# Sums of log f as spread rows, a stacked rank-17 product, a step inside the log sigmoid, and one product for two stacked heads

## The chip, the core and the metric

The kernel runs on one core of a Trainium2 chip. The metric is the device time of one execution in microseconds (us); lower is better. Engines are named as the profile names them: PE is TensorE (matmul), PEld its weight load, DVE is VectorE, ACT is ScalarE, POOL is GpSimd, SP is SyncE, which issues most of the DMA transfers.

## The reference, cut to what matters

Two layers of a decoder trunk over 256 positions of width 2048. Each layer normalises, projects to the columns of four head groups (four heads of width 128 each), runs four kinds of attention, gates them and maps back; a last RMSNorm follows. The change touches the forgetting attention, the gate of the gated linear attention (GLA) and GLA's product across chunks.

```python
log_f = jax.nn.log_sigmoid((p["fox_f"] + fox_fb).astype(jnp.float32)).transpose(0, 2, 1)
# forgetting attention: logit[t, s] = q_t.k_s / sqrt(d) + F[t] - F[s], F = cumsum(log f), causal
cum = jnp.cumsum(log_f.astype(jnp.float32), axis=-1)
logits = jnp.einsum("bhqd,bhkd->bhqk", q_i, k, preferred_element_type=jnp.float32) * scale
logits = logits + c_i[..., :, None] - cum[:, :, None, :]
...
# gated linear attention: the gate's logits are a product of rank 16 plus a bias (17 rows)
a_logit = jnp.einsum("bsr,re->bse", p["gla_a"], gla_wa2) + gla_ba
log_a = jax.nn.log_sigmoid(a_logit.astype(jnp.float32)) / GLA_TAU
```

The softmax takes no notice of a term that is the same for all keys of a row, so only the part of the sums that changes with the key `s` has to be added to the scores.

## The kernel before

**The stream.** All weights come in a list of steps, `plan`. For each step SP loads 512 or 348 KB into one of four buffers (`raw`); ScalarE writes the high part (`hi`, float32r), VectorE the rest (`lo = raw - hi`), and TensorE multiplies hi and lo with the high and low parts of the transposed activations (`hTp`, later `mTh` and `mTl`): `mm` is the usual PSUM tile of these products, `side` one of two PSUM tiles for everything else. The parts are made three steps ahead (`prepare`, `PART_BUFS` 4). A step of 512 columns is eight products with hi and four with lo.

**The side work.** Attention, norms and transposes are Python generators in the list `tasks`. After each step `tick` lets them run, one `yield` at a time, as long as the estimated time of VectorE and ScalarE (`Costed`) stays under what the products of the step give; so a piece of code between two `yield`s is issued together, and the order of all engines is fixed when the program is built. A key in `ready` tells one task that another has issued its result. Slots `s4` (ten tiles of 128x1024), `s2` (six of 128x512) and `s8` are handed out in the same way.

**log f.** `gla_gate` reads the four columns `fox_f` of both query blocks into `fx` and starts `fox_forget`: VectorE adds the bias, `log_sigmoid` runs Abs, Exp and Ln on ScalarE, and VectorE subtracts. `f` is split into `fh` and `fl`; ScalarE scales the constant triangles `since` by each head's column into two tiles of 128x1024. In `softmax_part` the object `forget` (class `Forget`) puts two products of a matrix of ones (`ones_r`) with these tiles in front of the score products of each key block, so the sums along the keys arise in PSUM.

**The gate.** `gla_first` reads the 16 columns `gla_a` into `an`; `gla` transposes them on TensorE, VectorE copies 16 rows into `at17`, whose row 17 holds ones, and two float32 products with `wa` (17 rows: `gla_wa2` and `gla_ba`) give the logits, which `log_sigmoid` takes further.

**GLA across chunks.** For each pair of heads, `ee[:, 0, NL]` and `ee[:, 1, NL]` hold the decayed k and q of two heads, 64 rows each; two products on rows 0 to 63 and 64 to 127 give `px`.

**The first norm.** `first_rms` squares the transposed x, adds it up into two tiles (`xts[0]`, `xts[3]`), and for each query block two products with a column of ones add up both.

`turned` is the pattern by which a tile is turned: VectorE transposes squares of 32, SP writes to the far memory (`far`), POOL reads back, and `LANDS` = 4 yields pass before the tile is used.

Of the kernel before, what the change touches and what calls it, by code (L numbers as in the profile page):

```python
# [208 lines left out]
def hybrid_trunk(  # L209
# [140 lines left out]
    wa = cp.tile([17, DEPTH, 256], F32, name="wa")  # L350
    ones_r = cp.tile([P, P], F32R, name="ones_r")
# [3 lines left out]
    at17 = cp.tile([17, SEQ], F32, name="at17")  # L355
# [17 lines left out]
    nc.vector.memset(at17, 1.0)  # L373

    def constants():
# [3 lines left out]
        nc.scalar.dma_start(wa[0:16], gla_wa2.rearrange("l r e -> r l e"))  # L379
        nc.scalar.dma_start(wa[16:17].rearrange("p l e -> p (l e)"), gla_ba.rearrange("(o l) e -> o (l e)", o=1))  # L380
# [15 lines left out]
        v_.tensor_scalar(ones_r, ident, 0.0, 1.0, op0=OP.mult, op1=OP.add)  # L396
        s4.put(mb)
        ready.add("constants")
# [131 lines left out]
    def log_sigmoid(dst, xin, e):  # L530

        a_.activation(e, xin, AF.Abs)
        a_.activation(e, e, AF.Exp, scale=-1.0)
        a_.activation(e, e, AF.Ln, bias=1.0)
        yield
        v_.scalar_tensor_tensor(dst, xin, 0.0, e, op0=OP.min, op1=OP.subtract)


    def gla_first(l, ps):
        r = env["r", l]  # L540
        an = sm.tile([P, 2, 16], F32, name="an", bufs=2)
        sg = sgs.get([P, 2, GW])
        env["gla_sg", l] = sg
        for m in range(2):
            a_.activation(an[:, m], ps[m][:, 0:16], AF.Copy, scale=r[:, m:m + 1])
            a_.activation(sg[:, m, :332], ps[m][:, 16:], AF.Silu, scale=r[:, m:m + 1])
        tasks.append(gla(l, an))
# [22 lines left out]
    def gla_gate(l, ps):  # L570
# [8 lines left out]
        env["forget", l] = Forget()  # L579
        tasks.append(fox_forget(l, fx, env["forget", l]))  # L580
# [11 lines left out]
    def gla(l, an):  # L592
        yield from until("constants")
        ps = yield from take_side()
        for m in range(2):
            transpose(ps[0:16, m * P:(m + 1) * P], an[:, m])
        yield
        v_.tensor_copy(at17[0:16], ps[0:16, 0:256])
        side.put(ps)
        yield  # L600
        al = yield from take_side()
        for pair in range(2):
            matmul(al[:, pair * SEQ:(pair + 1) * SEQ], wa[:, l, pair * P:(pair + 1) * P], at17, True, True)
# [21 lines left out]
        for pair in range(2):  # L625
# [34 lines left out]
            v_.tensor_mul(ee[:, 1, NL], ee[:, 1, NL], qv[:, 1])  # L660
# [19 lines left out]
            for hh in range(2):  # L680
                rows = slice(hh * 64, hh * 64 + 64)
                matmul(px[:, hh * 512:hh * 512 + P], ee[rows, 0, NL], ee[rows, 1, NL], True, True, tiles=2)
            s8.put(ee)
            yield
            a_.activation(sx[:, pair * 2:pair * 2 + 2], px.rearrange("p (h t) -> p h t", h=2)[:, :, :P], AF.Copy)
# [19 lines left out]
    def softmax_part(m, qT, kT, rows, scale, su, forget=None):  # L705
# [3 lines left out]
        for kt in range(m + 1):  # L709
            dst = S[:, kt]  # L710
            if forget is not None:
                forget(dst, kt)
            for h in range(H):
                matmul(dst[:, h], qT[rows, m * H + h], kT[1][rows, kt * H + h],
                       forget is None, forget is None or h == H - 1)
        yield
        v_.tensor_add(S[:, m], S[:, m], neg4)
        mx = sm.tile([P, H], F32, name="mx")
# [25 lines left out]
    def attend(l, gi, name, qT, kT, forget=None):  # L744
# [4 lines left out]
        for m, pool in enumerate((s2, s4)):  # L749
            p = yield from softmax_part(m, qT, kT, slice(0, P), HD ** -0.5, su, forget)  # L750
            if m:
                s4.put(qT, kT[0])
                if forget is not None:
                    forget.release()
# [40 lines left out]
    class Forget:  # L795

        def __init__(self):
            self.fg = []  # L800

        def __call__(self, dst, kt):
            matmul(dst, ones_r, self.fg[0][:, kt], True, False)
            matmul(dst, ones_r, self.fg[1][:, kt], False, False)

        def release(self):
            s4.put(*self.fg)

# [6 lines left out]
    def fox_forget(l, fx, forget):  # L815
        yield
        v_.tensor_add(fx, fx, fb[:, l, None, :].to_broadcast([P, 2, H]))
        e = sm.tile([P, 2, H], F32, name="fe", bufs=2)
# [4 lines left out]
        fh = sm.tile([P, 2, H], F32R, name="fh", bufs=2)  # L823
        fl = sm.tile([P, 2, H], F32R, name="fl", bufs=2)
        hi_of(fh, f)
        lo_of(fl, f, fh)
# [475 lines left out]
```

## Time and profile before

| | before |
|---|---|
| median of 3 runs | 910.66 us (910.32 to 911.14) |
| the profiled execution | 910.05 us |
| its span, first to last instruction | 908.3 us |
| mean granted clock of TensorE | 0.997 |
| instructions: PE, DVE, ACT, POOL | 4489, 833, 827, 55 |
| DMA queues: the share of 16 engines that SP's queue (q1) takes | 61.5% |
| table loads on ScalarE | 26 of 1.28 us under the helper's line, 1 at the start |

In the timeline of the profile a row is a run of like instructions on one engine: start, duration, engine, line, operation, tiles written and read, weights' shape, moving shape, count, and in brackets the idle time ahead and what ended it. The duration of a run of products includes the filling of the array, so the distance from one start to the next is what it takes from the stream. A float32 product appears as two records in the trace, a float32r product as one. Nearly all lines are those of helpers (L277 `matmul`, L179 the costed call), so groups are told apart by their tiles.

### The profile page before, as it was taken

How to read it: one execution, taken by the hardware profiler on the slowest of the kernel's cores; microseconds unless marked ns; L12 is line 12 of the kernel's file. 1: busy time of each engine (PE TensorE's matmuls, PEld its weight loads, DVE VectorE, ACT ScalarE, POOL GpSimd, SP SyncE). 2: the span in 40 equal slices, each digit the busy share in tenths (PEclk: the TensorE clock that was granted, in tenths of full speed). 3: DMA queues.
4: the chain of work that ended last, by engine and by line, in shares of the span. 5: the costliest groups of instructions: out<-in, count | busy, mean ns of one | idle time of the engine just before them, and what ended most of it. 6: DMA issues, size and time to landing. Idle time of an engine off the chain costs nothing.

```text
span 908.3 us, 12430 instructions
## 1 busy us (share of the span) xinstructions
PE 898.7 (99%) x4489; PEld 765.0 (84%) x4489; DVE 570.2 (63%) x833; ACT 530.9 (58%) x827; POOL 36.3 (4%) x55
## 2 busy tenths in 40 slices
PE   9999999999999999999999999999999999999996
PEld 7988889888888888888899888988888888888886
DVE  6764878466668555646655568766655684665662
ACT  7678654654656555535565785547645644754451
POOL 0000000000000010000000000000000000110000
PEclk9999999999999999999999999999999999999998
DMA  8857767479656947858776466674967588497652
GB/s 280 271 209 247 253 195 249 143 240 337 230 189 211 315 146 238 293 189 273 222 233 213 147 235 205 188 239 139 346 232 233 176 260 282 151 309 270 183 176 93
DMA packets 77743, 205.34 MB, mean 226 GB/s; under 512 B 9297, under 2 KB 29425, under 8 KB 77682
## 3 DMA queue, kind: packets, MB, share of 16 engines
q1 hardware_dynamic: 70640, 183.42, 61.5%
q0 software_dynamic: 5408, 19.40, 6.0%
q10 hardware_dynamic: 1634, 1.73, 0.6%
q8 instruction: 35, 0.57, 0.3%
q14 instruction: 26, 0.21, 0.1%
HBM read 184.07 MB, written 20.45 MB: 225 GB/s over the span
## 4 chain that ended last, share of the span: by engine, by line
PE 97%; ACT 1%; issue 1%; DVE 0%; POOLq 0%; POOL 0%; DVEq 0%; ACTq 0%
PE mm L277 87%; PE side L277 10%; PE side L369 0%; ACT L179 0%; ACT hi L179 0%; ACT two L179 0%; DVE two L179 0%; DVE xs L179 0%; POOLq L1298 0%; ACT four L179 0%; POOL rf L424 0%; ACT fe L179 0%; DVEq L1298 0%; PE side L281 0%; ACT gate L179 0%
## 5 line engine op out<-in xcount | busy, mean ns | idle before, releaser
L179 DVE TENSOR_TENSOR lo<-raw,hi 128x1024 fp32r<-128x1024 f32 (+2 forms) x319 | 368.0, 1160 | 299.9 <-ACT hi L179 288.4
L179 ACT ACTIVATE hi<-raw 128x1024 fp32r<-128x1024 f32 (+2 forms) x319 | 319.6, 1009 | 295.5 <-PE mm L277 231.0
L277 PE MATMUL mm<-hi,hTp 128*128 128x512 f32 (+1 forms) x1920 | 461.1, 382 | 0.6 <-ACT hi L179 0.6
L277 PEld LDWEIGHTS mm<-hi,hTp 128*128 128x128 f32 x1920 | 351.1, 188 | 66.1 <-ACT hi L179 2.2
L277 PE MATMUL mm<-lo,hTp 128*128 128x512 f32 (+1 forms) x960 | 248.1, 380 | 0.0
L277 PEld LDWEIGHTS mm<-lo,hTp 128*128 128x128 f32 x960 | 177.4, 188 | 32.8
L277 PE MATMUL mm<-hi,mTh 128*128 128x512 f32 (+1 forms) x256 | 64.6, 377 | 0.0
L277 PE MATMUL mm<-hi,mTl 128*128 128x512 f32 (+1 forms) x256 | 64.4, 376 | 0.0
L277 PE MATMUL mm<-lo,mTh 128*128 128x512 f32 (+1 forms) x256 | 64.4, 376 | 0.0
L277 PEld LDWEIGHTS mm<-lo,mTh 128*128 128x128 f32 x256 | 46.2, 188 | 8.8
L277 PEld LDWEIGHTS mm<-hi,mTl 128*128 128x128 f32 x256 | 46.2, 188 | 8.8
L277 PEld LDWEIGHTS mm<-hi,mTh 128*128 128x128 f32 x256 | 46.1, 188 | 8.6
L313 POOL DMA_DIRECT2D four<-far x32 | 17.2, 539 | 598.9 <-DMA far<-four 243.4
L277 PE MATMUL side<-four,four 128*128 128x128 f32 (+1 forms) x320 | 37.0, 276 | 0.0
L277 PEld LDWEIGHTS side<-four,four 128*128 128x128 f32 (+1 forms) x320 | 34.1, 190 | 2.3 <-issue 1.4
L179 ACT ACT_TABLE_LOAD x26 | 33.4, 1283 | 0.4
L179 DVE STREAM_TRANSPOSE four<-four 128x1024 f32<-128x1024 f32 x24 | 29.5, 1231 | 0.0
L179 ACT ACTIVATE four<-mm,rstd 128x512 f32<-128x512 f32 (+1 forms) x40 | 24.4, 661 | 0.1
L277 PE MATMUL side<-hi,hTp 128*128 128x348 f32 x128 | 23.1, 321 | 0.0
L277 PEld LDWEIGHTS side<-hi,hTp 128*128 128x128 f32 x128 | 20.9, 188 | 1.4 <-issue 0.7
L179 ACT ACTIVATE four<-side,nb 128x256 f32<-128x256 f32 (+1 forms) x48 | 20.5, 439 | 1.3 <-DVE nb L179 1.2
L179 ACT ACTIVATE four<-side 32x64 f32<-32x64 f32 (+2 forms) x28 | 8.8, 342 | 18.2 <-PE side L277 17.9
(135 smaller groups left out, 498.5 us busy)
## 6 DMA issues: line engine op xcount, KB each, us to landing
raw<-in_weights SPq DMA_DIRECT2D x271, 512.0 KB, 4.3
far<-four SPq DMA_DIRECT2D x128, 128.0 KB, 4.4
four<-far POOLq DMA_DIRECT2D x32, 512.0 KB, 5.9
raw<-in_weights SPq DMA_DIRECT2D x46, 348.0 KB, 3.7
xs<-in_x SPq DMA_DIRECT2D x4, 512.0 KB, 5.0
four<-in_xt SPq DMA_DIRECT2D x3, 512.0 KB, 5.8
far<-two SPq DMA_DIRECT2D x24, 64.0 KB, 4.2
two<-far POOLq DMA_DIRECT2D x6, 256.0 KB, 5.3
```

The source lines that it names most:

```text
L179: return f(*args, **kw)
L277: t_.matmul(out, lhsT, rhs, start=start, stop=stop)
L313: g_.dma_start(t, d.rearrange("j c i f -> (j c) (i f)"))
```

## The change

Six edits. (1) The sums of log f: two products of `f` with the triangles give one row of sums per head (4 rows); VectorE copies them, SP writes them to the far memory, POOL reads them back spread over all 128 partitions into one tile, and VectorE adds this tile to the scores. The class `Forget`, `ones_r` and the 32 scaled copies go. (2) The rank-17 product: `an` holds the 16 columns and a one three times, in strips of 32; the product is one float32r product over 128 rows, with strips high·high, low·high and high·low. (3) A `yield` between VectorE's addition and Abs, one between Exp and Ln, and more of them around the sums and the gate. (4) GLA's two products become one of 256 columns whose moving tile `qx` has zeros where the rows belong to the other head. (5) The first norm adds both tiles on VectorE and needs one product for each query block. (6) Memsets of the new tiles, and six transfers for `wa`'s strips instead of two.

```diff
@@ -349,4 +349,3 @@
     gng = cp.tile([P, DEPTH], F32, name="gng")
-    wa = cp.tile([17, DEPTH, 256], F32, name="wa")
-    ones_r = cp.tile([P, P], F32R, name="ones_r")
+    wa = cp.tile([P, DEPTH, 256], F32R, name="wa")
     neg_b = cp.tile([P, P], BF16, name="neg_b")
@@ -354,3 +353,5 @@
     halfpow = cp.tile([P, 8], F32, name="halfpow")
-    at17 = cp.tile([17, SEQ], F32, name="at17")
+    at = cp.tile([P, SEQ], F32R, name="at")
+    an = cp.tile([P, 2, 4, 32], F32, name="an")
+    qx = cp.tile([P, 2, P], F32, name="qx")
     lam = cp.tile([P, DEPTH], F32, name="lam")
@@ -372,3 +373,2 @@
     keep_warm(WARM)
-    nc.vector.memset(at17, 1.0)
 
@@ -378,4 +378,7 @@
         nc.scalar.dma_start(ct, const)
-        nc.scalar.dma_start(wa[0:16], gla_wa2.rearrange("l r e -> r l e"))
-        nc.scalar.dma_start(wa[16:17].rearrange("p l e -> p (l e)"), gla_ba.rearrange("(o l) e -> o (l e)", o=1))
+        w3 = s2.get([P, DEPTH, 256])
+        g_.memset(w3, 0.0)
+        for i in range(0, 96, 32):
+            nc.scalar.dma_start(w3[i:i + 16], gla_wa2.rearrange("l r e -> r l e"))
+            nc.scalar.dma_start(w3[i + 16:i + 17].rearrange("p l e -> p (l e)"), gla_ba.rearrange("(o l) e -> o (l e)", o=1))
         yield
@@ -395,4 +398,7 @@
         v_.tensor_copy(masks.rearrange("p l t -> p (l t)"), mb)
-        v_.tensor_scalar(ones_r, ident, 0.0, 1.0, op0=OP.mult, op1=OP.add)
         s4.put(mb)
+        hi_of(wa, w3)
+        yield
+        lo_of(wa[64:96], w3[64:96], wa[64:96])
+        s2.put(w3)
         ready.add("constants")
@@ -533,2 +539,3 @@
         a_.activation(e, e, AF.Exp, scale=-1.0)
+        yield
         a_.activation(e, e, AF.Ln, bias=1.0)
@@ -540,3 +547,2 @@
         r = env["r", l]
-        an = sm.tile([P, 2, 16], F32, name="an", bufs=2)
         sg = sgs.get([P, 2, GW])
@@ -544,5 +550,5 @@
         for m in range(2):
-            a_.activation(an[:, m], ps[m][:, 0:16], AF.Copy, scale=r[:, m:m + 1])
+            a_.activation(an[:, m, 0:3, 0:16], ps[m][:, None, 0:16].to_broadcast([P, 3, 16]), AF.Copy, scale=r[:, m:m + 1])
             a_.activation(sg[:, m, :332], ps[m][:, 16:], AF.Silu, scale=r[:, m:m + 1])
-        tasks.append(gla(l, an))
+        tasks.append(gla(l))
 
@@ -578,4 +584,3 @@
         env["fox_v", l] = vn
-        env["forget", l] = Forget()
-        tasks.append(fox_forget(l, fx, env["forget", l]))
+        tasks.append(fox_forget(l, fx))
 
@@ -591,3 +596,3 @@
 
-    def gla(l, an):
+    def gla(l):
         yield from until("constants")
@@ -595,10 +600,12 @@
         for m in range(2):
-            transpose(ps[0:16, m * P:(m + 1) * P], an[:, m])
+            transpose(ps[:, m * P:(m + 1) * P], an[:, m].rearrange("p a r -> p (a r)"))
         yield
-        v_.tensor_copy(at17[0:16], ps[0:16, 0:256])
+        v_.tensor_copy(at, ps[:, :SEQ])
+        lo_of(at[32:64], ps[32:64, :SEQ], at[32:64])
         side.put(ps)
         yield
+        yield
         al = yield from take_side()
         for pair in range(2):
-            matmul(al[:, pair * SEQ:(pair + 1) * SEQ], wa[:, l, pair * P:(pair + 1) * P], at17, True, True)
+            matmul(al[:, pair * SEQ:(pair + 1) * SEQ], wa[:, l, pair * P:(pair + 1) * P], at, True, True)
         yield
@@ -659,3 +666,5 @@
             v_.tensor_mul(ee[:, 0, NL], ee[:, 0, NL], kv[:, 0])
-            v_.tensor_mul(ee[:, 1, NL], ee[:, 1, NL], qv[:, 1])
+            for hh in range(2):
+                rows = slice(hh * 64, hh * 64 + 64)
+                v_.tensor_mul(qx[rows, hh], ee[rows, 1, NL], qv[rows, 1])
             yield
@@ -679,8 +688,6 @@
             px = yield from take_side()
-            for hh in range(2):
-                rows = slice(hh * 64, hh * 64 + 64)
-                matmul(px[:, hh * 512:hh * 512 + P], ee[rows, 0, NL], ee[rows, 1, NL], True, True, tiles=2)
+            matmul(px[:, :2 * P], ee[:, 0, NL], qx.rearrange("p h t -> p (h t)"), True, True)
             s8.put(ee)
             yield
-            a_.activation(sx[:, pair * 2:pair * 2 + 2], px.rearrange("p (h t) -> p h t", h=2)[:, :, :P], AF.Copy)
+            a_.activation(sx[:, pair * 2:pair * 2 + 2], px[:, :2 * P].rearrange("p (h t) -> p h t", h=2), AF.Copy)
             side.put(px)
@@ -709,10 +716,8 @@
         for kt in range(m + 1):
-            dst = S[:, kt]
-            if forget is not None:
-                forget(dst, kt)
             for h in range(H):
-                matmul(dst[:, h], qT[rows, m * H + h], kT[1][rows, kt * H + h],
-                       forget is None, forget is None or h == H - 1)
+                matmul(S[:, kt, h], qT[rows, m * H + h], kT[1][rows, kt * H + h], True, True)
         yield
         v_.tensor_add(S[:, m], S[:, m], neg4)
+        if forget is not None:
+            v_.tensor_add(S[:, :m + 1], S[:, :m + 1], forget[:, :m + 1])
         mx = sm.tile([P, H], F32, name="mx")
@@ -753,3 +758,3 @@
                 if forget is not None:
-                    forget.release()
+                    s4.put(forget)
             v_.reciprocal(rs[:, m], su[:, m])
@@ -794,16 +799,2 @@
 
-    class Forget:
-
-
-
-        def __init__(self):
-            self.fg = []
-
-        def __call__(self, dst, kt):
-            matmul(dst, ones_r, self.fg[0][:, kt], True, False)
-            matmul(dst, ones_r, self.fg[1][:, kt], False, False)
-
-        def release(self):
-            s4.put(*self.fg)
-
     def fox_v(l, ps):
@@ -814,5 +805,6 @@
 
-    def fox_forget(l, fx, forget):
+    def fox_forget(l, fx):
         yield
         v_.tensor_add(fx, fx, fb[:, l, None, :].to_broadcast([P, 2, H]))
+        yield
         e = sm.tile([P, 2, H], F32, name="fe", bufs=2)
@@ -822,15 +814,21 @@
         yield
-        fh = sm.tile([P, 2, H], F32R, name="fh", bufs=2)
-        fl = sm.tile([P, 2, H], F32R, name="fl", bufs=2)
-        hi_of(fh, f)
-        lo_of(fl, f, fh)
-        yield
-        for part in (fh, fl):
-            z = yield from s4.take([P, 2, H, P], F32R)
-            pf = part.bitcast(F32)
-            for m in range(2):
-                for h in range(H):
-                    a_.activation(z[:, m, h], since[m], AF.Copy, scale=pf[:, m, h:h + 1])
-            forget.fg.append(z)
+        yield
+        yield
+        ps = yield from take_side()
+        for m in range(2):
+            matmul(ps[:H, m * P:(m + 1) * P], f[:, m], since[m], True, True)
+        yield
+        c = sm.tile([H, 2, P], F32, name="cum", bufs=2)
+        v_.tensor_copy(c, ps[:H, :SEQ].rearrange("h (m s) -> h m s", m=2))
+        side.put(ps)
+        yield
+        d = yield from far.take([1, 2, H, P])
+        nc.sync.dma_start(d[0].rearrange("m h s -> h m s"), c)
+        yield
+        z = yield from s4.take([P, 2, H, P])
+        g_.dma_start(z.rearrange("p m h s -> p (m h s)"), d.rearrange("o m h s -> o (m h s)").to_broadcast([P, 2 * H * P]))
+        far.put(d)
+        for _ in range(LANDS):
             yield
+        env["forget", l] = z
         ready.add(("forget", l))
@@ -1147,2 +1145,3 @@
                 fold(xts[0 if c == 2 else 3])
+        v_.tensor_add(xts[0][:, 0], xts[0][:, 0], xts[3][:, 0])
         yield
@@ -1151,4 +1150,3 @@
         for m in range(2):
-            for c in (0, 3):
-                matmul(ps[:, m:m + 1], xts[c][:, 0, m * P:(m + 1) * P], one, c == 0, c == 3)
+            matmul(ps[:, m:m + 1], xts[0][:, 0, m * P:(m + 1) * P], one, True, True)
         t = before_pow(ps[:, 0:2], 2, 1.0 / D)
@@ -1249,2 +1247,5 @@
     g_.memset(tq, 0.0)
+    g_.memset(qx, 0.0)
+    g_.memset(an, 0.0)
+    g_.memset(an[:, :, 0:3, 16:17], 1.0)
     tasks += [constants()]
```

Three places show how the order moves. On TensorE in the first layer, the gate (`an` transposed by `ct`, then `at` with `wa`) before:

```order
L281 MATMUL side_612<-ct,an 16x128 x2
L277 MATMUL mm<-hi,hTp 128x512 x8
L277 MATMUL mm<-lo,hTp 128x512 x4
L277 MATMUL side_210<-hi,hTp 128x348 x8
L277 MATMUL side_210<-lo,hTp 128x348 x4
L277 MATMUL side_661<-at_91,wa 128x256 x2
```

and now:

```order
L281 MATMUL side_638<-ct,an 128x128 x2
L277 MATMUL side_213<-hi,hTp 128x348 x8
L277 MATMUL side_213<-lo,hTp 128x348 x4
L277 MATMUL side_213<-hi,hTp 128x348 x8
L277 MATMUL side_213<-lo,hTp 128x348 x4
L277 MATMUL mm<-hi,hTp 128x512 x8
L277 MATMUL mm<-lo,hTp 128x512 x4
L277 MATMUL side_725<-at,wa 128x256 x2
```

The product with `wa` moves behind a step of 512 columns, and the transposes fill 128 rows instead of 16.

On TensorE in the first layer, the scores of the forgetting attention for the second query block (`four,ones_r` are the rows of log f, `four,four` queries and keys) before:

```order
L277 MATMUL mm<-lo,hTp 128x512 x4
L277 MATMUL side_1771<-four_823,ones_r 128x512
L277 MATMUL side_1771<-four_850,ones_r 128x512
L277 MATMUL side_1771<-four_1404,four_1312 128x128 x4
L277 MATMUL side_1771<-four_823,ones_r 128x512
L277 MATMUL side_1771<-four_850,ones_r 128x512
L277 MATMUL side_1771<-four_1404,four_1312 128x128 x4
```

and now, with the score products of the first query block ten rows ahead:

```order
L277 MATMUL side_1569<-four_1374,four_1322 128x128 x4
L277 MATMUL mm<-hi,hTp 128x512 x8
L277 MATMUL mm<-lo,hTp 128x512 x4
L277 MATMUL mm<-hi,hTp 128x512 x8
L277 MATMUL mm<-lo,hTp 128x512 x4
L277 MATMUL mm<-hi,hTp 128x512 x8
L277 MATMUL mm<-lo,hTp 128x512 x4
L277 MATMUL mm<-hi,hTp 128x512 x8
L277 MATMUL mm<-lo,hTp 128x512 x4
L277 MATMUL side_1672<-four_1374,four_1322 128x128 x8
```

The rows of ones are gone, the score products stand together, and four steps instead of five lie between the two query blocks.

On ScalarE in the second layer, the log sigmoid of log f (`fx` to `fe`: Abs, Exp, Ln) among the high parts before:

```order
L179 ACTIVATE four_4444<-side_4043,rstd 128x164
L179 ACTIVATE hi<-raw 128x1024
L179 ACTIVATE fe<-fx 128x8
L179 ACT_TABLE_LOAD
L179 ACTIVATE fe<-fe 128x8
L179 ACT_TABLE_LOAD
L179 ACTIVATE fe<-fe 128x8
L179 ACTIVATE hi<-raw 128x1024 x2
L179 ACTIVATE fh<-f 128x8
```

and now, with the end of the gate's log sigmoid (`two`) ahead of it:

```order
L179 ACTIVATE two_4452<-two_4452 128x512
L179 ACTIVATE hi<-raw 128x1024
L179 ACT_TABLE_LOAD
L179 ACTIVATE two_4452<-two_4452 128x512
L179 ACTIVATE hi<-raw 128x1024
L179 ACTIVATE fe<-fx 128x8
L179 ACT_TABLE_LOAD
L179 ACTIVATE fe<-fe 128x8
L179 ACTIVATE hi<-raw 128x1024
L179 ACT_TABLE_LOAD
L179 ACTIVATE fe<-fe 128x8
L179 ACTIVATE hi<-raw 128x1024 x3
```

A high part now stands between Exp and Ln of either log sigmoid.

## The prediction

> **What bounds the kernel now.** I read the page's head first, then the chain that ended last, then what TensorE and ScalarE waited for, and last TensorE's timeline around each place that the change touches.
>
> ```profile
> span 908.3 us, 12430 instructions
> PE 898.7 (99%) x4489; PEld 765.0 (84%) x4489; DVE 570.2 (63%) x833; ACT 530.9 (58%) x827; POOL 36.3 (4%) x55
> PE 97%; ACT 1%; issue 1%; DVE 0%; POOLq 0%; POOL 0%; DVEq 0%; ACTq 0%
> PE mm L277 <- ACT hi L179: 0.6, 1, 0.6
> ACT hi L179 <- PE mm L277: 231.0, 155, 3.9
> ```
>
> TensorE is busy 99% of the span and carries 97% of the chain. Once the projections run, the only wait of TensorE is one of 0.6 us, while ScalarE waits 231.0 us for TensorE before it may write the next high part. So the time is the length of TensorE's instruction stream: what leaves it is gained in full, what joins it is paid in full, and work on the other engines is free until a weight part comes late. A busy time overlaps its neighbours, so I take every price from start to start. The rhythm of a step is the unit:
>
> ```profile
> 508.66 1.98 PE L277 MATMUL mm<-hi,hTp 128*128 128x512 f32 x8
> 510.47 1.07 PE L277 MATMUL mm<-lo,hTp 128*128 128x512 f32 x4
> 511.38 1.98 PE L277 MATMUL mm<-hi,hTp 128*128 128x512 f32 x8
> ```
>
> Eight products take 1.81 us and four take 0.91: a step of twelve is 2.72 us. Where a group of four or eight takes longer than that, the insertion beside it is charged with the excess.
>
> **The rows of log f (TensorE, both layers).** Before, each key block of the scores begins with two products of the ones matrix.
>
> ```profile
> 164.54 0.64 PE L277 MATMUL side<-four,ones_r 128*128 128x512 f32 x2
> 165.02 1.05 PE L277 MATMUL side<-four,four 128*128 128x128 f32 x8
> ...
> 179.55 0.64 PE L277 MATMUL side<-four,ones_r 128*128 128x512 f32 x2
> ...
> 180.84 0.71 PE L277 MATMUL side<-four,ones_r 128*128 128x512 f32 x2
> ...
> 182.19 2.09 PE L277 MATMUL mm<-hi,hTp 128*128 128x512 f32 x8
> 333.64 1.95 PE L277 MATMUL side<-four,four 128*128 128x128 f32 x16
> 335.35 2.10 PE L277 MATMUL mm<-hi,hTp 128*128 128x512 f32 x8
> ```
>
> For the first query block they take 165.02 - 164.54 = 0.48 us. For the second, the whole group takes 182.19 - 179.55 = 2.64; the MoBA scores of the same shape, which have no such rows, take 335.35 - 333.64 = 1.71 for their 16 instructions. So 0.48 + 0.93 = 1.41 a layer goes, **-2.8 us** in two. In their place come two float32 products with 4-column weights and 128 moving columns a layer. No row has that form. Each float32 product is two instructions here (eight scores, 16 records); at 1.71 / 16 = 0.107, and 0.111 with the 0.04 lost at the group's edge, four cost 0.45 to 0.5: **+1.0 us**. The bounds are 4 x 0.07 (a transpose with few columns, below) and 4 x 0.26 (the dearest float32 row below): +0.6 to +2.1.
>
> The rest of this part leaves TensorE. The 32 scaled copies on ScalarE go; VectorE gets an addition of the table to the scores, 512 and 1024 elements wide. The same engine adds the mask at 0.69 us for 512, so a layer pays 0.69 + about 1.4 = 2.1:
>
> ```profile
> L179 DVE TENSOR_TENSOR side<-side,neg_b 128x512 f32<-128x512 f32 x12 | 8.3, 692 | 5.5 <-PE side L277 5.5
> far<-four SPq DMA_DIRECT2D x128, 128.0 KB, 4.4
> two<-in_final_norm_g POOLq DMA_DIRECT2D x4, 256.0 KB, 9.5
> ```
>
> I cost it at nothing: VectorE is idle 37% of the span and in each step has 2.72 us for one low part. If that cover were gone, 4.2 us would join the path. The addition also waits for the table's round trip, 4.4 us to the far memory and, as a spread row, some 9.5 to twice that back: 14 to 23 us. Queued behind it on VectorE are the low parts. But between the copy of the sums and the addition stand 25 low parts in VectorE's order, one a step, some 68 us. On SP's queue the write of the sums stands between weight loads, and waits for a VectorE copy made one turn earlier; the turned tiles' writes stand there in the same way today. On POOL's queue the spreading read stands between two reads like it.
>
> **The rank-17 product.**
>
> ```profile
> 500.89 1.42 PE L277 MATMUL side<-hi,hTp 128*128 128x348 f32 x8
> 502.15 0.79 PE L277 MATMUL side<-lo,hTp 128*128 128x348 f32 x4
> 502.87 1.13 PE L277 MATMUL side<-at,wa 17*128 17x256 f32 x4
> 503.93 1.52 PE L277 MATMUL side<-hi,hTp 128*128 128x348 f32 x8
> 505.29 0.79 PE L277 MATMUL side<-lo,hTp 128*128 128x348 f32 x4
> 895.14 0.28 PE L277 MATMUL side<-four,mTl 128*128 128x256 f32 x1
> 895.26 0.40 PE L277 MATMUL side<-four,mTh 128*128 128x256 f32 x2
> 895.50 0.28 PE L277 MATMUL side<-four,mTl 128*128 128x256 f32 x1
> ```
>
> Two float32 products, four instructions, take 503.93 - 502.87 = 1.06 us (0.26 each). They also stretch their neighbours: eight of 348 columns take 1.26 ahead and 1.36 behind, and the four between take 0.72 where half of 1.26 is 0.63. Together 1.25. After, there are two float32r products with 256 moving columns and 128 rows, one instruction each; three such take 895.50 - 895.14 = 0.36, so two take 0.24. That is 1.0 a layer, **-2.0 us**. The bounds: if the new product kept the old price per instruction, 2 x 0.26, it would be -1.5.
>
> The transposes ahead of it now load 128 columns of weights instead of 16, and the square sums of the first norm lose one of two products:
>
> ```profile
> 46.40 0.95 PE L277 MATMUL side<-one,four 128*128 128x1 f32 x8
> 47.21 1.50 PE L277 MATMUL mm<-hi,hTp 128*128 128x348 f32 x8
> 51.92 0.38 PE L281 MATMUL side<-ct,an 128*16 128x128 f32 x2
> 52.06 2.07 PE L277 MATMUL mm<-hi,hTp 128*128 128x512 f32 x8
> ```
>
> Eight square-sum instructions take 47.21 - 46.40 = 0.81, so half is **-0.4 us**. Two transposes take 0.14; with full weights I give each the 0.10 of a square-sum instruction, which has full weights and one moving column: 0.20, **+0.1 us** in two layers. The Trainium skill ("TensorE: Matmul & The Clock Gate", LDWEIGHTS) prices a weight load by its columns at 1.2 per ns, 107 ns for 128 against 13 for 16; by that the two layers would pay about 0.4. The trace agrees for full weights: the square-sum instructions come every 0.10 us.
>
> **The stacked rows' product.** Two products on 64 rows become one on 128 rows, whose other half is zeros, with twice the columns.
>
> ```profile
> 116.93 1.08 PE L277 MATMUL mm<-lo,hTp 128*128 128x512 f32 x4
> 117.94 0.49 PE L277 MATMUL side<-eight 64*128 64x128 f32 x4
> 118.36 2.11 PE L277 MATMUL mm<-hi,hTp 128*128 128x512 f32 x8
> 120.31 1.07 PE L277 MATMUL mm<-lo,hTp 128*128 128x512 f32 x4
> 250.42 1.16 PE L277 MATMUL side<-four,four 64*128 64x128 f32 x16
> 251.51 2.11 PE L277 MATMUL mm<-hi,hTp 128*128 128x512 f32 x8
> ```
>
> Before, the pair takes 118.36 - 117.94 = 0.42, the four ahead 1.01 instead of 0.91 and the eight behind 1.95 instead of 1.81: 0.66. After, two instructions of 256 columns at twice 0.111, with 0.04 for the edge: 0.48. Four pairs: **-0.7 us**; at 0.26 each it is -0.4.
>
> Against this edit speaks a rule of the Trainium skill ("TensorE: Matmul & The Clock Gate", Part 3): small products on different row groups run at the same time, and a short contraction costs as much as a full one. The trace agrees where the run is long: 16 instructions of 64 rows take 251.51 - 250.42 = 1.09, or 0.068 each against 0.107. What it does here is a rival below.
>
> **The step between the instructions (and the queues).** The one wait of TensorE is at 520:
>
> ```profile
> 518.63 1.07 PE L277 MATMUL mm<-lo,hTp 128*128 128x512 f32 x4
> 520.25 2.12 PE L277 MATMUL mm<-hi,hTp 128*128 128x512 f32 x8 [0.56 <-ACT hi L179]
> 516.00 0.21 ACT L179 ACTIVATE fe<-fx 128x8 f32<-128x8 f32 x1 [2.69 <-DVE fx L179]
> 519.16 1.99 ACT L179 ACTIVATE hi<-raw 128x1024 fp32r<-128x1024 f32 x2
> ```
>
> ScalarE stood 2.69 us at Abs, waiting for VectorE's addition, then ran Abs, Exp and Ln with two table loads up to 519.16, and only then wrote the high part that TensorE needed. In the new order a high part stands on either side of Exp and ahead of Abs, and the addition is issued a turn ahead of Abs. Four of the group took 1.62 us instead of 0.91: **-0.7 us** if nothing takes its place. What is late next is the high part after the two table loads of the rank-17 product's log sigmoid; there too a high part now stands between the loads. The constants issue four more transfers on ScalarE's queue near 40 us, some 2 us by their spacing in the trace (0.5), where ScalarE later idles 2.0 us for TensorE: nothing.
>
> **Sum:** -2.8 + 1.0 - 2.0 - 0.4 + 0.1 - 0.7 - 0.7 = **-5.5 us**. The profiled execution took 910.05 us, 1.75 more than its span; 904.5 follows for one like it. The median of the three runs is 0.61 higher, so I forecast **905.1 us**.
>
> **Rivals.**
> 1. *A new late part.* The side work now starts several steps earlier in the stream, as the order shows, and ScalarE's or VectorE's burst may meet a due part elsewhere. For it: a wait of 0.56 already cost 0.7. Against it: ScalarE loses 32 copies and four table loads. The gain of 0.7 stays out and one or two waits come at 0.7 each: 906 to 907.
> 2. *The 64-row pairs were cheap.* If two products overlapped wholly, as the long run suggests, and the edges came from elsewhere, a pair cost 4 x 0.068 = 0.27 and its successor 0.48: +0.8 instead of -0.7, 906.6. This is what the Trainium skill's rule above gives here ("TensorE: Matmul & The Clock Gate", Part 3).
> 3. *The change does not do what it says on TensorE:* the stacked product and the sums' product run at 0.26 an instruction. The first loses 0.5 and the second adds 1.1: 906.7.
> 4. *Slower: the spread table comes late.* VectorE stands at the addition with the low parts behind it. TensorE has three steps ahead, 8 us. To lose the 4.8 us that the other terms give (5.5 less the 0.7 at 520), each layer must wait 2.4 us beyond these 8, so the table must land 68 + 8 + 2.4 = 78 us after the copy. The round trip is 14 to 23. If it took 85, the time would be 910.66 - 4.8 + 2 x 9 = 924.
>
> **How the numbers follow.** Forecast 0.62, rival 1 0.15, rival 2 0.10, rival 3 0.05, rival 4 0.04; 0.04 is left for a gain that other waits eat up to within 0.2% (1.8 us), about what a measurement of this kernel can tell from no change. The kind end of the sums' products, +0.6, gives 904.7, and the runs of before lie up to 0.5 from their median: from 904.1 down to 904.0. Rivals 1 to 3 end at 907, with the same spread 907.4. The range 904.0 to 907.4 leaves out rival 4, the rest and a little on either side. Faster 0.91, same 0.05, slower 0.04.
>
> **What would show it.** The ones rows gone from the groups and MoBA-like groups of 8 and 16 in the FoX scores; groups for the sums at 0.45 to 0.5 a layer; two products of 256 columns in 0.24; a 256-column product of the stacked rows in 0.45; no wait of TensorE on ScalarE near 520. I am wrong if TensorE's waits exceed 1 us in sum, if VectorE waits for the table, or if the sums' products take more than 0.7 us.

## The result and the profile after

The changed kernel takes **905.56 us** (median of four runs, 905.17 to 906.74) against 910.77 for the kernel before on the same chip (910.32 to 911.14): a ratio of 0.9945, with a 95% interval of 0.9928 to 0.9962, so 5.2 us less. The profiled execution of the changed kernel took 906.74 us (span 905.0), the slowest of its four; the one of before took 910.05. What the two traces differ by, 3.3 us, is therefore less than what the medians differ by, and a part of the reading below is why.

The head of the page after (busy time and share of each engine, then the shares of the chain that ended last):

```profile
span 905.0 us, 12378 instructions
PE 894.0 (99%) x4469; PEld 762.8 (84%) x4469; DVE 579.2 (64%) x843; ACT 518.0 (57%) x790; POOL 40.3 (4%) x61
PE 97%; DMA 1%; issue 1%; DVE 0%; ACT 0%; ACTq 0%; POOLq 0%; POOL 0%; DVEq 0%; SPq 0%
```

TensorE still sets the time: 99% busy, 97% of the chain. ScalarE lost 13 us of work and VectorE gained 9, and neither shows in the chain. What TensorE waited for (in total, times, longest):

```profile
PE side L277 <- DVE four L179: 1.3, 1, 1.3
PE side L370 <- DVE one L365: 1.2, 1, 1.2
PE mm L277 <- ACT hi L179: 0.2, 1, 0.2
```

The second row is the warm-up before the first projection, at the start of the span; before had the same. The third is the first projection's own start: 0.24 us at 5.45, where only the warm-up had run. The first is new. TensorE's timeline (start, duration, line, operation, and in brackets the idle time ahead) at the places that the change touches:

```profile
46.19 0.79 PE L277 MATMUL mm<-lo,hTp 128*128 128x348 f32 x4
48.26 0.58 PE L277 MATMUL side<-one,four 128*128 128x1 f32 x4 [1.28 <-DVE four L179]
48.70 1.51 PE L277 MATMUL mm<-hi,hTp 128*128 128x348 f32 x8
...
81.32 1.07 PE L277 MATMUL mm<-lo,hTp 128*128 128x512 f32 x4
82.32 0.60 PE L277 MATMUL side<-ct,f 128*4 128x128 f32 x4
82.85 2.11 PE L277 MATMUL mm<-hi,hTp 128*128 128x512 f32 x8
84.80 1.07 PE L277 MATMUL mm<-lo,hTp 128*128 128x512 f32 x4
...
112.49 1.08 PE L277 MATMUL mm<-lo,hTp 128*128 128x512 f32 x4
113.41 0.59 PE L277 MATMUL side<-qx,eight 128*128 128x256 f32 x2
113.65 2.21 PE L277 MATMUL mm<-hi,hTp 128*128 128x512 f32 x8
115.70 1.07 PE L277 MATMUL mm<-lo,hTp 128*128 128x512 f32 x4
...
166.08 1.95 PE L277 MATMUL side<-four,four 128*128 128x128 f32 x16
167.78 2.10 PE L277 MATMUL mm<-hi,hTp 128*128 128x512 f32 x8
...
497.13 0.38 PE L281 MATMUL side<-ct,an 128*128 128x128 f32 x2
497.26 2.11 PE L277 MATMUL mm<-hi,hTp 128*128 128x512 f32 x8
499.21 1.08 PE L277 MATMUL mm<-lo,hTp 128*128 128x512 f32 x4
...
503.90 0.40 PE L277 MATMUL side<-at,wa 128*128 128x256 f32 x2
504.13 2.01 PE L277 MATMUL mm<-hi,hTp 128*128 128x512 f32 x8
505.98 1.07 PE L277 MATMUL mm<-lo,hTp 128*128 128x512 f32 x4
...
519.58 1.07 PE L277 MATMUL mm<-lo,hTp 128*128 128x512 f32 x4
520.48 1.98 PE L277 MATMUL mm<-hi,hTp 128*128 128x512 f32 x8
```

Read from start to start, with 0.91 for four and 1.81 for eight as the undisturbed rhythm:

| place | before | after |
|---|---|---|
| square sums: group / four of 348 columns ahead | 0.81 / 0.63 | 0.44 / 2.07 |
| sums' products, with both edges, a layer | none | 0.53 + 0.09 + 0.14 = 0.76 |
| product of stacked heads, with edges | 0.66 | 0.24 + 0.01 + 0.24 = 0.49 |
| FoX scores, second query block | 2.64 | 1.70 |
| two transposes, second layer, with the edge behind | 0.13 + 0.10 = 0.23 | 0.13 + 0.14 = 0.27 |
| gate's product, with edges | 1.25 | 0.23 + 0.04 = 0.27 |
| wait near 520 (four products with lo) | 1.62 | 0.90 |

The new wait is 2.07 - 0.63 = 1.44 us, ahead of the first norm's square sums. They need VectorE's additions (`four`), and those need squares that ScalarE writes. ScalarE's timeline there (ACTq rows are its issues of transfers, ACT rows its computing):

```profile
40.46 0.79 ACT L179 ACTIVATE hi<-raw 128x696 fp32r<-128x696 f32 x1 [1.13 <-PE mm L277]
...
40.84 0.44 ACTq L382 DMA_DIRECT2D two<-in_gla_wa  x1
...
42.57 0.95 ACTq L382 DMA_DIRECT2D two<-in_gla_wa  x1
45.12 0.24 ACTq L383 DMA_DIRECT2D two<-in_gla_ba  x1
45.41 1.06 ACT L179 ACTIVATE four<-four 128x1024 f32<-128x1024 f32 x1 [4.16 <-DMA two<-in_gla_wa]
```

The six transfers of `constants` (two before) are issued from 40.84 on, every 0.3 to 0.6 us; then the queue stands from 43.5 to 45.12 at the sixth, and ScalarE computes nothing for 4.16 us. The squares come at 45.41, the additions end at 48.1, and TensorE has waited.

Of the table's way, three rows of VectorE's timeline, and then GpSimd's issue of the spreading read:

```profile
87.61 0.41 DVE L179 COPY cum<-side 4x256 f32<-4x256 f32 x1
...
156.54 0.70 DVE L179 TENSOR_TENSOR side<-side,four 128x512 f32<-128x512 f32 x1
...
170.56 1.23 DVE L179 TENSOR_TENSOR side<-side,four 128x1024 f32<-128x1024 f32 x1
```

```profile
93.91 0.54 POOL L829 DMA_DIRECT2D four<-far  x1 [18.29 <-DMA far<-cum]
```

The sums are copied at 87.61, the read that spreads them is issued at 93.91, and the first addition runs at 156.54 with no idle time ahead of it: 63 us lie between issue and addition.

The two traces now add up. From the first projection product (5.11 before, 5.45 after) to the last start of a matmul (900.18, 896.48) the stream is 895.07 long before and 891.03 after: 4.04 less, and 5.5 less without the wait of 1.44. The start is 0.34 later and the end, after that last matmul, 0.40 longer (8.12 before, 8.52 after); TensorE's work at neither is touched by the change, and the start lies anywhere from 5.11 to 6.16 in the traces quoted or used here.

### The profile page after: what moved, and what is told of

It is laid out like the page before. It is cut to its first block, busy times and chain, and to the rows that moved or that the text cites. A ratio compares the mean times of both kernels' runs of the same rounds, so it can differ in the third digit from the quotient of the medians.

```text
span 905.0 us, 12378 instructions
## 1 busy us (share of the span) xinstructions
PE 894.0 (99%) x4469; PEld 762.8 (84%) x4469; DVE 579.2 (64%) x843; ACT 518.0 (57%) x790; POOL 40.3 (4%) x61
## 4 chain that ended last, share of the span: by engine, by line
PE 97%; DMA 1%; issue 1%; DVE 0%; ACT 0%; ACTq 0%; POOLq 0%; POOL 0%; DVEq 0%; SPq 0%
PE mm L277 88%; PE side L277 9%; DMA raw<-in_weights 0%; DMA two<-in_gla_wa 0%; DVE four L179 0%; ACT four L179 0%; DVE xs L179 0%; ACT hi L179 0%; ACTq L383 0%; ACTq L382 0%; POOLq L1299 0%; POOL rf L430 0%; ACT two L179 0%; DVEq L1299 0%; PE side L281 0%
## 5 line engine op out<-in xcount | busy, mean ns | idle before, releaser
L179 ACT ACTIVATE four<-four 128x1024 f32<-128x1024 f32 x14 | 14.8, 1058 | 10.1 <-DMA four<-far 5.3
```

Source lines behind the costliest of these rows:

```text
L179: return f(*args, **kw)
```

## The experiments

The theory after the result: the terms on TensorE's stream are as priced, but for the sums' products, whose 4-column weights cost edges; and the constants' transfers in ScalarE's queue hold up the squares. The rivals: the wait comes from something else that moved (other weight loads, VectorE's additions), the step inside the log sigmoid is what matters, the pairs of 64 rows were cheap. Ratios are against the runs of the kernel before on the same chip, with medians of 910.25 to 910.50 (910.77 for the result above). So medians of kernels from different sets of runs may differ by 0.5 us from this alone; where the text subtracts such medians, the difference is no more than a hint, and the reading rests on the traces.

**Two transfers instead of six.** The strips of `wa` are written from one copy on the chip.

```diff
-        for i in range(0, 96, 32):
-            nc.scalar.dma_start(w3[i:i + 16], gla_wa2...)
-            nc.scalar.dma_start(w3[i + 16:i + 17]..., gla_ba...)
+        nc.scalar.dma_start(w3[0:16], gla_wa2...)
+        nc.scalar.dma_start(w3[16:17]..., gla_ba...)
...
         hi_of(wa, w3)
+        hi_of(wa[32:64], w3[0:32])
...
-        lo_of(wa[64:96], w3[64:96], wa[64:96])
+        lo_of(wa[64:96], w3[0:32], wa[0:32])
```

> The changed kernel, but wa's strips come by two transfers instead of six; ScalarE and VectorE make the second and third strip from the first. Theory (the new wait of TensorE ahead of the square sums, a gap of 2.07 us where 0.63 is usual, comes from ScalarE's queue, which stood at the last of the six transfers until an earlier transfer had landed): the wait goes, ScalarE's idle time of 4.2 us ahead of the first norm's squares goes, 905.6 - 1.4 = 904.2 us. Rival (the added VectorE addition of 0.42 us makes the square sums late by itself): TensorE still waits, 0.4 us or more, 904.6 to 905.6.

904.90 us (904.58 to 906.90), ratio 0.9941 [0.9928, 0.9954]. Two rows of TensorE's timeline in this run:

```profile
46.10 0.79 PE L277 MATMUL mm<-lo,hTp 128*128 128x348 f32 x4
46.73 0.50 PE L277 MATMUL side<-one,four 128*128 128x1 f32 x4
```

The wait is gone: 0.63 for the four ahead. ScalarE now idles 0.65 us ahead of the squares, not 4.16. The median falls by 0.7, not by the 1.44 of the one trace, and the two intervals overlap. That the wait differs from trace to trace, the next kernels show. One of the five runs here took 906.90 and has no trace, so the transfers may not be all that makes a run longer.

**The same six transfers, issued by GpSimd.**

```diff
-            nc.scalar.dma_start(w3[i:i + 16], gla_wa2...)
-            nc.scalar.dma_start(w3[i + 16:i + 17]..., gla_ba...)
+            g_.dma_start(w3[i:i + 16], gla_wa2...)
+            g_.dma_start(w3[i + 16:i + 17]..., gla_ba...)
```

> The changed kernel with all six transfers for wa issued by GpSimd instead of ScalarE. Theory (the wait ahead of the square sums comes from ScalarE's queue standing at a transfer, not from the transfers themselves): ScalarE idles under 1 us ahead of the first norm's squares, no wait of TensorE there, 904.9 us as with two transfers. Rival (the six transfers are late or hold the memory whichever queue issues them): a wait of TensorE between 40 and 65 us stays, 905.6 us or more.

904.74 us (904.57 to 905.17), 0.994 [0.9926, 0.9953], with no wait of TensorE ahead of the square sums. ScalarE's squares follow the high part without idle time:

```profile
40.83 0.79 ACT L179 ACTIVATE hi<-raw 128x696 fp32r<-128x696 f32 x1 [1.13 <-PE mm L277]
...
41.52 1.04 ACT L179 ACTIVATE four<-four 128x1024 f32<-128x1024 f32 x1
```

The number of transfers is the same as in the changed kernel, only their queue is another. So it is ScalarE's queue that carried the cost, not the transfers as such.

**The rows of ones back.** The class `Forget`, `ones_r` and the 32 scaled copies of before return; all else stays.

```diff
+            if forget is not None:
+                forget(dst, kt)
...
-        if forget is not None:
-            v_.tensor_add(S[:, :m + 1], S[:, :m + 1], forget[:, :m + 1])
...
-            matmul(ps[:H, m * P:(m + 1) * P], f[:, m], since[m], True, True)
...
+                    a_.activation(z[:, m, h], since[m], AF.Copy, scale=pf[:, m, h:h + 1])
```

> The changed kernel with the rows of ones and the 32 scaled copies back in place of the spread table; all other edits stay. Theory (TensorE's stream decides): plus 2.8 us for the rows of ones, minus 2 x 0.76 us for the sums' products as the trace of after shows them, so 905.6 + 1.3 = 906.9 us, no new wait of TensorE. Rival (the 32 copies that left ScalarE are what keeps the high parts on time): in addition a wait of TensorE on ScalarE between 55 and 90 us or between 500 and 535 us of 0.5 us or more, 907.5 us or above.

906.91 us (906.00 to 907.99), 0.9958 [0.9946, 0.997]: 1.35 over the changed kernel, which is 2 x 1.41 less 2 x 0.76 = 1.3. The wait at the square sums is 0.43 us here, with ScalarE idle 3.15 ahead of the squares.

**The rank-17 product back**, in float32 on 17 rows, with its two transfers straight into `wa`.

```diff
-    wa = cp.tile([P, DEPTH, 256], F32R, name="wa")
+    wa = cp.tile([17, DEPTH, 256], F32, name="wa")
...
-            transpose(ps[:, m * P:(m + 1) * P], an[:, m].rearrange("p a r -> p (a r)"))
+            transpose(ps[0:16, m * P:(m + 1) * P], an[:, m])
...
-            matmul(al[:, ...], wa[:, l, pair * P:(pair + 1) * P], at, True, True)
+            matmul(al[:, ...], wa[:, l, pair * P:(pair + 1) * P], at17, True, True)
```

> The changed kernel with the float32 product over 17 rows and its two transfers back; all other edits stay. Theory: plus 2.0 us for the product (1.25 instead of 0.24 us a layer), minus 1.4 us for the wait ahead of the square sums, which the six transfers cause: 905.6 + 0.6 = 906.2 us. Rival (that wait has another cause): 907.6 us, with the wait still there.

906.60 us (906.54 to 907.44), 0.9956 [0.9944, 0.9968]. In its trace the product takes 1.05 us in the second layer:

```profile
501.23 1.12 PE L277 MATMUL side<-at,wa 17*128 17x256 f32 x4
502.28 1.52 PE L277 MATMUL side<-hi,hTp 128*128 128x348 f32 x8
```

Against the kernel with two transfers and the stacked product, the fair partner since neither has the wait at the square sums, it is 1.7 us slower, where the sum gave 2.0.

**Both steps inside the log sigmoid taken out.**

```diff
         a_.activation(e, e, AF.Exp, scale=-1.0)
-        yield
         a_.activation(e, e, AF.Ln, bias=1.0)
...
         v_.tensor_add(fx, fx, fb[:, l, None, :].to_broadcast([P, 2, H]))
-        yield
```

> The changed kernel without the two steps (none between VectorE's addition and Abs, none between Exp and Ln). Theory (the step is what removed TensorE's wait near 520 us): a wait of TensorE on ScalarE returns in the second layer, the gap of 1.62 instead of 0.91 us, 905.6 + 0.7 = 906.3 us. Rival (the order of the gate and the missing copies already leave ScalarE ahead): no wait, 905.6 us, and four more table loads on ScalarE at most.

906.04 us (twelve timings, 904.95 to 913.77), 0.9958 [0.9943, 0.9973]; the profiled one is the fastest. ScalarE's timeline at the second layer's log sigmoid, and TensorE's beside it:

```profile
511.57 0.21 ACT L179 ACTIVATE fe<-fx 128x8 f32<-128x8 f32 x1 [2.09 <-DVE fx L179]
...
513.10 0.21 ACT L179 ACTIVATE fe<-fe 128x8 f32<-128x8 f32 x1
...
514.62 0.21 ACT L179 ACTIVATE fe<-fe 128x8 f32<-128x8 f32 x1
```

```profile
515.00 1.07 PE L277 MATMUL mm<-lo,hTp 128*128 128x512 f32 x4
515.91 2.01 PE L277 MATMUL mm<-hi,hTp 128*128 128x512 f32 x8
```

ScalarE stands 2.09 us for VectorE's addition and runs the burst in one piece, with a table load of 1.28 us at each of the two places left out, as before; yet TensorE keeps 0.91 for its four. The theory that the step is what keeps the wait away falls. The wait at the square sums is absent in this trace too, although the six transfers are still there: ScalarE idles 2.34 us ahead of the squares, which is short enough.

**The kernel before with only those two steps added** (the same two lines, as additions).

> The kernel before with the two steps alone (between VectorE's addition and Abs, between Exp and Ln). Theory (the step by itself takes away TensorE's wait near 520 us): the gap there is 0.91 us again, 910.5 - 0.7 = 909.8 us. Rival (the place of the gate's product in the order did it, the step nothing): the wait of some 0.6 us stays, 910.5 us.

909.69 us (ten timings, 908.92 to 913.35), 0.9995 [0.9985, 1.0004]: no difference that can be told. The profiled execution is the slowest of the ten; its projections begin 1.05 us later than before's. TensorE's timeline in it:

```profile
518.58 1.07 PE L277 MATMUL mm<-lo,hTp 128*128 128x512 f32 x4
519.49 1.98 PE L277 MATMUL mm<-hi,hTp 128*128 128x512 f32 x8
...
537.62 1.07 PE L277 MATMUL mm<-lo,hTp 128*128 128x512 f32 x4
538.87 2.12 PE L277 MATMUL mm<-hi,hTp 128*128 128x512 f32 x8 [0.18 <-ACT hi L179]
540.82 1.07 PE L277 MATMUL mm<-lo,hTp 128*128 128x512 f32 x4
542.51 2.11 PE L277 MATMUL mm<-hi,hTp 128*128 128x512 f32 x8 [0.62 <-ACT hi L179]
```

Near 520 the four take 0.91, so the step alone is enough there. But a wait comes at 538 and 542, where four take 1.25 and 1.69. The span of this trace is 3.2 us longer than before's, and 2.9 of that are lost by the square sums near 49, ahead of both log sigmoids; so it needn't stand for the other nine executions. ScalarE's scaled copies, which the change removes, lie there (from 532.14 and from 543.30 on), and ahead of them it stands 5.28 us for a turned tile's read from the far memory. The kernel with the rows of ones back has the same copies in the same order and stood 1.38 us at that place. The row of this kernel, then that of the kernel with the rows of ones:

```profile
531.17 1.06 ACT L179 ACTIVATE four<-four 128x1024 f32<-128x1024 f32 x1 [5.28 <-DMA four<-far]
```

```profile
522.07 1.06 ACT L179 ACTIVATE four<-four 128x1024 f32<-128x1024 f32 x1 [1.38 <-DMA four<-far]
```

There TensorE waits nowhere from 505 to 549: each four of 512 columns takes 0.91. So the copies alone don't bring the wait. It stays away with the copies and the later gate (rows of ones back), and with the early gate and no copies (the rank-17 product back, 0.90 or 0.91 for each four).

**Two transfers, the rows of ones back, no steps.** What is left of the change is the stacked gate, the pairs' product and the square sums.

```diff
-        yield
         a_.activation(e, e, AF.Ln, bias=1.0)
...
+            if forget is not None:
+                forget(dst, kt)
...
+        nc.scalar.dma_start(w3[0:16], gla_wa2...)
```

> The changed kernel with two transfers for wa, with the rows of ones and the scaled copies back, and without the two steps: of what could have removed the wait near 520 us only the gate's later place is left. Theory (that place is enough): no wait of TensorE there, 904.9 + 1.3 = 906.2 us. Rival (one of the steps or the missing copies is needed): a gap of about 1.6 instead of 0.91 us in the second layer, 906.9 us.

907.11 us (906.69 to 908.46), 0.9966 [0.9953, 0.998]. Near 520 the excess is 0.07 us, and one gap of 0.21 appears at 535; so the later place of the gate's product and its log sigmoid nearly suffices by itself. That rests on the trace: the time is 0.9 above what I expected and would fit the rival's 906.9 as well. Against the first experiment's trace 0.25 of it lies at the start and 0.28 in those two gaps; the rest is not accounted for.

**The sums' weights padded to 128 columns** with zeros; 128 rows of sums are formed and four are read.

```diff
+    fw = cp.tile([P, 2, P], F32, name="fw")
...
-        v_.tensor_scalar(f, f, math.sqrt(HD), None, op0=OP.mult)
+        v_.tensor_scalar(fw[:, :, 0:H], f, math.sqrt(HD), None, op0=OP.mult)
...
-            matmul(ps[:H, m * P:(m + 1) * P], f[:, m], since[m], True, True)
+            matmul(ps[:, m * P:(m + 1) * P], fw[:, m], since[m], True, True)
```

> The changed kernel with the sums' weights padded with zeros from 4 to 128 columns; the extra rows of the result are not used. Theory (weights narrower than the array cost an edge on both sides, as 64 and 17 rows do: 0.53 us and 0.09 ahead and 0.14 behind): the group takes about 0.45 and nothing ahead, 0.2 to 0.3 us a layer less, 905.6 - 0.5 = 905.1 us, or 904.5 where the wait ahead of the square sums does not fall. Rival (the price is that of four float32 instructions between float32r ones, whatever their width): 0.53 and 0.23 stay, 905.6 us.

905.72 us (904.58 to 906.73), 0.9949 [0.9934, 0.9963]; its profiled execution has 1.80 us of wait at the square sums (ScalarE idle 4.52), which hides the small gain in the median. TensorE's timeline at the sums:

```profile
81.61 1.08 PE L277 MATMUL mm<-lo,hTp 128*128 128x512 f32 x4
82.53 0.61 PE L277 MATMUL side<-ct,fw 128*128 128x128 f32 x4
82.89 2.08 PE L277 MATMUL mm<-hi,hTp 128*128 128x512 f32 x8
84.81 1.07 PE L277 MATMUL mm<-lo,hTp 128*128 128x512 f32 x4
```

0.36 for the group, 0.01 ahead and 0.11 behind: 0.48 instead of 0.76. Thirty-two times the weights cost less. Of the 0.28 saved, 0.17 lie in the group itself and 0.11 at its edges.

**The table added twice, half of it each time**, 3.9 us more on VectorE over two layers.

```diff
-            v_.tensor_add(S[:, :m + 1], S[:, :m + 1], forget[:, :m + 1])
+            for _ in range(2):
+                v_.tensor_add(S[:, :m + 1], S[:, :m + 1], forget[:, :m + 1])
...
-        v_.tensor_scalar(f, f, math.sqrt(HD), None, op0=OP.mult)
+        v_.tensor_scalar(f, f, 0.5 * math.sqrt(HD), None, op0=OP.mult)
```

> The changed kernel with half the table added twice to the scores: four more additions on VectorE, 2 x (0.70 + 1.23) = 3.9 us. Theory (VectorE's additions are hidden by TensorE's stream): 905.6 us as the change, no new wait of TensorE. Rival (the additions stand on the path): 909.5 us.

905.58 us (904.96 to 906.71), 0.9949 [0.9934, 0.9964]; TensorE waits 0.3 us in the stream, at its start. The additions are hidden, and so is as much again.

**Two transfers, and the two 64-row products back.**

```diff
-            matmul(px[:, :2 * P], ee[:, 0, NL], qx.rearrange("p h t -> p (h t)"), True, True)
+            for hh in range(2):
+                rows = slice(hh * 64, hh * 64 + 64)
+                matmul(px[:, hh * 512:hh * 512 + P], ee[rows, 0, NL], ee[rows, 1, NL], True, True, tiles=2)
```

> The changed kernel with two transfers for wa and the two 64-row products for each pair of heads back in place of the one of 256 columns. Theory (a pair costs 0.66 us with its edges, the single product 0.48): 904.9 + 0.7 = 905.6 us, the pair 0.42 with 1.01 ahead and 1.95 behind. Rival (two products on different row groups overlap, so a pair costs half of what one product of 256 columns does): 904.9 - 0.8 = 904.1 us.

905.43 us (905.34 to 906.00), 0.9948 [0.9936, 0.996]: 0.5 over the first experiment (0.6 by the ratios) for four pairs, where the rows give 4 x 0.17 = 0.7. These read as before the change: 0.42 for the pair, 1.01 ahead, 1.95 behind. A lone pair of 64-row products isn't cheap.

**Two transfers and the padded sums together.**

> The changed kernel with two transfers for wa and with the sums' weights padded to 128 columns: both things that the runs found against the change are taken out. Expected: 904.9 - 0.56 = 904.3 us, 0.993 of before, no wait of TensorE after the first products of the stream. If the gains do not add, 904.9 us.

**904.45 us** (904.20 to 905.06), 0.9936 [0.9922, 0.995], the fastest of all, 1.1 under the changed kernel and 0.45 under the first experiment (as much by the ratios, whose intervals overlap); 2 x 0.28 = 0.56 was expected. Its trace has both gains: 0.63 for the four ahead of the square sums, and 0.37 and 0.36 for the two groups of the sums.

## Why the prediction was right, and where it was not

The direction and the mechanism held: the time is the length of TensorE's stream. The forecast was 0.5 us under the median, because two errors of the working went against it (+0.5 for the sums' products and up to 1.4 for a wait), and small things went for it. That these nearly made up for each other is luck. By its own signs the text was wrong twice: TensorE's new wait is 1.28 us in the one trace, where the sign was 1 us, and the sums' products take more than 0.7.

- **The rows of ones: right.** The scores' groups read like MoBA's (1.70 for 16), and putting the rows back costs 1.35 net.
- **The sums' products: mis-sized.** The term was "+1.0 us", at 0.45 to 0.5 a layer, and the text called itself wrong above 0.7. It is 0.76, so +1.5. Two parts failed. The four instructions take 0.53, not 4 x 0.107 = 0.43; and "the 0.04 lost at the group's edge" is 0.23. The padded kernel brings these to 0.36 and 0.12. The rows of before held the warning: the eight behind the first block's scores, which have full weights, start at 165.82 and the next group at 167.76, 1.94 for 1.81, so even there the edge was 0.13; and the edges of the pairs and of the rank-17 product I had put down to few rows alone.
- **The rank-17 product: right.** 0.27 with edges against 1.25; putting it back costs 1.7 of the 2.0.
- **The transposes: nothing in the group itself instead of "+0.1".** They take 0.13 with 128 weight columns and took 0.13 to 0.14 with 16. The eight behind them take 1.95 instead of 1.91 in the second layer, so some 0.04 of the 0.06 a layer that were counted may have joined the stream there (in the first layer a group of another width stands behind). The 0.4 that the two layers would pay by the price of the Trainium skill ("TensorE: Matmul & The Clock Gate", LDWEIGHTS) isn't seen here.
- **The square sums: right** in length (0.36 to 0.44 for the group).
- **The pairs: right in sum, by luck in its parts.** 0.49 against "0.48", and 905.43 against 904.90 when undone. But the two instructions take 0.24, where 2 x 0.222 was counted, and the edges 0.25 instead of 0.04. Rival 2 is out by its own numbers: the pair's edges stay with the pair. For the rule that speaks against it (the Trainium skill, the same page, Part 3), two products are too few to pay for their edges: the long run of 16 instructions has edges of the same size (1.00 ahead, 1.95 behind in the trace of before) and spreads them over 16.
- **The wait near 520: gone as said, the reason only half right.** "A high part stands on either side of Exp" was given as the cause. It is sufficient (the steps alone clear 520) and not necessary (without the steps 520 stays clear, by the gate's later place). Alone it gains nothing that can be told. Its one trace has waits at 538 and 542; with the steps and either the gate's later place or the copies gone, no trace has them. Why they came there (the copies together with the 5.28 us that ScalarE stood ahead of them, or that one execution) stays open.
- **The constants' transfers: the failed step.** "Nothing", since ScalarE idles 2.0 us later. The text counted the six issues at 0.5 us each and put them against idle time that lies behind the squares. It did not ask what is queued behind them: the squares, for which TensorE waits. And the issues did not all follow each other every 0.3 to 0.6 us: the last ones stood. ScalarE's idle time ahead of the squares was 2.3, 2.3, 3.15, 4.16 and 4.5 us in five traces with the six transfers, and TensorE's wait none, none, 0.43, 1.44 and 1.80; in all five traces with the two transfers it was 0.65 and none. From some 3 us on the cover is gone. So rival 1, a new late part, came in as well, at a place that it did not name. Which earlier transfer holds the queue isn't settled: the releaser that the profile names is `two` in two of the traces and a weight load in two others.
- **VectorE's additions and the table: right.** Twice the additions cost nothing, and VectorE waited at no addition, so rival 4 did not come near its point of decision. Rival 3 is out at 0.12 and 0.13 an instruction.

With the measured prices the sum is -2.8 + 1.5 - 2.0 - 0.4 - 0.7 - 0.7 = -5.1 us, and the wait of nothing to 1.8 comes on top, from trace to trace. The medians lie 5.2 apart. The stream in the one trace lost 5.5 besides the wait, so some 0.4 of small gains has no term of its own; where they lie stays open.

## What to carry to other kernels

In these traces an issue of a transfer holds its place in its engine's queue (the squares at 45.41 stood behind the issue at 45.12): before one is added, look at what computing stands behind it there, and who waits for that, not at how idle the engine is on the whole. A small product between long groups is priced with its edges, from the start of the neighbour ahead to the start of the group after the neighbour behind; filling its rows and columns with zeros can be cheaper than leaving them out (0.48 against 0.76 here). And when a wait is gone from one place, look for it at the next ones: the kernel with the steps alone had none at 520 and two behind it.

## What was not expected of the hardware

- Four float32 instructions with 4 weight columns cost 0.76 us between long groups, and 0.48 with 128 columns of which 124 are zeros.
- Two transposes with 128 weight columns were no longer from start to start than with 16: 0.13 against 0.14 us, and 0.04 more on the eight products behind.
- With the same six issues on ScalarE's queue it computed nothing for between 2.3 and 4.5 us, in five traces of five kernels that differ elsewhere; with them on GpSimd's queue, in one trace, neither its squares nor TensorE waited.
- One float32r product of 256 columns on 128 rows (0.12 us) replaced two float32 instructions of 17 rows (0.53).
